# Moving the two-input steps of the projection's GpSimd share to VectorE in a hybrid SGU, convolution and RWKV7 block

## The chip, the cores and the metric

The kernel runs on one core of a Trainium2 chip. The time is that of one execution on the device, in microseconds (us), and a kernel is described by the median of several executions. The engines are TensorE (PE in the rows, PEld for its weight loads), VectorE (DVE), ScalarE (ACT), GpSimd (POOL) and SyncE (SP, which issues the DMAs). A queue works its instructions off in order: one that waits holds all that stand behind it on its engine.

## The reference

The block takes 2048 tokens of width 1024, normalises them, projects them to 29 x 128 columns, feeds three branches, and projects back:

```python
h = rms_norm(x, pre_norm_g[i])
z = h @ w_in[i]                                   # 1024 x 3712
out_a = spatial_gating(u_a, v_a, ...) * silu(g_a)
out_b = conv_module(val_b, glu_b, ...) * silu(g_b)        # 31-tap depthwise convolution
out_c = rwkv7_mix(z[..., oc:og], ...) * silu(z[..., og:]) # token shift, low-rank decay, scan
mix = concatenate([out_a, out_b, out_c]) @ w_out[i]
x = x + rms_norm(mix, post_norm_g[i])
gate = sigmoid(x @ ple_gate_w[i] + ple_gate_b[i])
x = x + (p[i] @ ple_w[i]) * gate
```

All is float32. The change is in how the operands of `z = h @ w_in` and of the low-rank step of `rwkv7_mix` are made ready.

## The kernel before

**Products in two parts.** To keep float32 accuracy, each operand is split in a high part, the value cast to the matmul's own format (a copy on ScalarE), and a low part, the value minus the high part. A product is then the sum of high x high, high x low and low x high. For one column tile (128 columns) over one half of the tokens (1024) that makes 2 groups of 512 tokens x 8 blocks x 3 products = 48 matmuls of 128x512 at line L300 (`gemm1`), some 11.2 us of PE.

**Loops.** The projection runs in two halves of 1024 tokens, each over 29 column tiles in the order of the list `ORDER`. In the first half, `load_w` loads a tile's weights (L278), casts the high part on ScalarE (L282), makes the low part (L283) and writes both to DRAM; in the second half `again` reads them back. Weights and parts share the buffers of the tag "w", six of them, two parts per tile. So the low part of a tile can be written when the gemm of the tile two places before it in `ORDER` has ended, and the load of its raw weights starts when the one three places before has. Accumulators (tag "z") have two buffers: the tile two places on may start when all that read the accumulator are done, for a shifted tile ScalarE's L329, VectorE's L330 and ScalarE's L336.

**Tokens.** The normalised tokens h come in four groups of 512. Group 0 is transposed on PE. Groups 1 to 3 are loaded transposed and scaled (L268), then split (L269, L270). `norm_h` puts the engine for L268 into the tuple `X[g]`: VectorE for group 2, GpSimd for groups 1 and 3.

**What stands around it.** While the projection runs, VectorE works off the 31-tap convolution (L443, then 30 steps L452 for each of two channel tiles and half), the token shift (L330) and the preparation of the RWKV7 operands for four pairs of heads (L469 to L553). The latter has chains across engines: ScalarE's L231 and VectorE's L232 split a tensor, L240 sums it on PE, VectorE's L245 takes reciprocals, and products (L505 to L553) follow. The low-rank part is split at L429 and L430. At the end of the second half L240 (on PE), L637 (ScalarE), L245 and L641 (VectorE) normalise the convolution's output.

**What sets the order.** Each step carries a priority (`at`, or the number that a generator yields, in units of column tiles), and a scheduler with a modelled timeline puts every engine's instructions in order from these priorities and its own idea of durations. The order on all engines can therefore change when a step changes engine. From the last six tiles of the second half on, PE's and VectorE's order is written by hand.

**What GpSimd does.** L165 (two lora weights' low parts), L268 for groups 1 and 3, L283, L430; besides them memsets, the copies L857 and L858, and the products L978 and L1108 of later stages.

Of the kernel before, what the change touches and what calls it, by code (L numbers as in the profile page):

```python
# [14 lines left out]
ALU = mybir.AluOpType  # L15
# [19 lines left out]
def hybrid_kernel(ctx, tc, x, x_t, w_in, vecs, wup, pw_w, sgu_wt, sgu_lnb, sgu_b,  # L35
# [115 lines left out]
    def s_const():  # L151
        yield -0.3
        nc.sync.dma_start(out=swt, in_=sgu_wt)
        nc.gpsimd.memset(swt[64:128, :, 0:64], 0.0)
        lnb = new("mk", (128, 256))
        nc.sync.dma_start(out=lnb, in_=sgu_lnb.partition_broadcast(128))
        sbr = new("mk", (1, 512))
        nc.sync.dma_start(out=sbr, in_=sgu_b)
        wup_t = new("mk", (128, 512))
        nc.sync.dma_start(out=wup_t, in_=wup)  # L160
        for j in range(2):
            hi = slice(64 * j, 64 * j + 64)
            for lo in (0, 64):
                nc.scalar.copy(wup_h[lo:lo + 64, j], wup_t[hi])
            nc.gpsimd.tensor_tensor(out=wup_l[hi], in0=wup_t[hi], in1=wup_h[hi, j], op=ALU.subtract)  # L165
        nc.sync.dma_start(out=pw_t, in_=pw_w.rearrange("(k p) n -> p k n", p=128))
        yield 1.5
        cps = mps((128, 2, 128))
        for hd in range(4):
            ct, lo = hd // 2, 64 * (hd % 2)  # L170
            nc.tensor.matmul(cps[lo:lo + 64, ct, :], lhsT=lnb[:, hd * 64:hd * 64 + 64], rhs=swt[:, hd, :],
                             start=True, stop=False)
            nc.tensor.matmul(cps[lo:lo + 64, ct, :], lhsT=mask[0:1, 64:128], rhs=sbr[:, hd * 128:hd * 128 + 128],
                             start=False, stop=True)
        nc.vector.tensor_copy(out=cmat, in_=cps)
# [12 lines left out]
    def norm_h(g):  # L188


        xt = []
        if g == 0:
            for i in range(4):
                if i == 1:
                    yield
                xi = new("L")
                nc.sync.dma_start(out=xi, in_=x[i * 128:(i + 1) * 128, :])
                junk = new("mk")
                rs = sb.tile([128, 2], F32, tag="rs1", bufs=2, name=nm("rs"))
                nc.scalar.activation(junk, xi, AF.Square, accum_out=rs[:, 0:1])  # L200
                rstd(rs[:, 1:2], rs[:, 0:1], 1.0 / D, 0, 1)
                nc.vector.tensor_scalar(out=xi, in0=xi, scalar1=rs[:, 1:2], scalar2=None, op0=ALU.mult)
                xt.append(xi)
            X[g] = xt
            return
        ssq = sb.tile([128, 4], F32, tag="ssq", bufs=2, name=nm("ssq"))
        for i in range(4):
            xi = new("L")
            nc.sync.dma_start(out=xi, in_=x[(4 * g + i) * 128:(4 * g + i + 1) * 128, :])
            nc.scalar.activation(xi, xi, AF.Square, accum_out=ssq[:, i:i + 1])  # L210
        rs = sb.tile([128, 4], F32, tag="rs", bufs=2, name=nm("rs"))
        rstd(rs, ssq, 1.0 / D, 0, 4)
        rb = new("mk", (128, 2, 512))
        rt = rb[:, 0].rearrange("p (i t) -> p i t", t=128)
        nc.vector.tensor_copy(out=rt, in_=rs.unsqueeze(2).to_broadcast([128, 4, 128]))
        tp = mps(tag="c")
        for i in range(4):
            nc.tensor.transpose(tp[:, i * 128:(i + 1) * 128], rt[:, i, :], ident)
        nc.scalar.copy(rb[:, 1], tp)
        for k2 in range(4):  # L220
            yield
            xk = new("L", (128, 2, 512))
            nc.sync.dma_start(out=xk, in_=x_t[256 * k2:256 * k2 + 256, g * 512:(g + 1) * 512]
                              .rearrange("(k p) t -> p k t", p=128))
            xt += [xk[:, 0], xk[:, 1]]
        X[g] = (xt, rb[:, 1], nc.vector if g % 2 == 0 else nc.gpsimd)

    def parts(src, eng):

# [17 lines left out]
    def build_h(xr, t):  # L247

        h = new("h", (128, 2, 8, 512), F32R)
        if len(xr) == 4:  # L250
# [11 lines left out]
                    nc.scalar.copy(h[:, 0, k4, sl], xb)  # L262
                    nc.vector.tensor_tensor(out=h[:, 1, k4, sl], in0=xb, in1=h[:, 0, k4, sl], op=ALU.subtract)
            return h
        xt, rb, eng = xr
        for k in range(8):
            at(t + 0.05 * k)
            eng.tensor_tensor(out=xt[k], in0=xt[k], in1=rb, op=ALU.mult)  # L268
            nc.scalar.activation(h[:, 0, k, :], xt[k], AF.Identity, scale=col(V_PRE + k))  # L269
            nc.vector.scalar_tensor_tensor(out=h[:, 1, k, :], in0=xt[k], scalar=col(V_PRE + k),  # L270
                                           in1=h[:, 0, k, :], op0=ALU.mult, op1=ALU.subtract)
        return h

    def load_w(*cts, tag="w"):
# [5 lines left out]
        for wr, ct in zip(wrs, cts):  # L280
            ws = [new("w", dt=F32R) for _ in range(2)]
            nc.scalar.copy(ws[0], wr)  # L282
            nc.gpsimd.tensor_tensor(out=ws[1], in0=wr, in1=ws[0], op=ALU.subtract)  # L283
            for j in range(2):
                nc.sync.dma_start(out=w_s[ct, :, j], in_=ws[j].bitcast(F32))
            r.append(ws)
# [130 lines left out]
    def s_lora(half, st):  # L417
# [8 lines left out]
        for j, tag in enumerate(("pg", "mk")):  # L426
            wa = new(tag, dt=F32R)
            hi, lo = slice(64 * j, 64 * j + 64), slice(64 - 64 * j, 128 - 64 * j)
            nc.scalar.copy(wa[hi], o[hi])  # L429
            nc.gpsimd.tensor_tensor(out=wa[lo], in0=o[hi], in1=wa[hi], op=ALU.subtract)  # L430
            st["wa"].append(wa)

    def s_conv(half, ct, st):
# [918 lines left out]
```

## Time and profile before

| | us |
|---|---|
| median of 3 runs | 1438.82 (1437.01 to 1440.38) |
| the profiled execution | 1437.73 |
| its span, first to last instruction | 1436.0 |
| PE busy | 1378.8 |
| VectorE busy | 1009.2 |
| ScalarE busy | 568.6 |
| GpSimd busy | 246.0 |

The mean granted clock of PE is 0.987 of full speed. Busy time is the sum over a whole execution. Which engine the others wait for changes from stretch to stretch, and so the views by stretch and the timelines are read beside it. In a timeline a row gives the start, the length of a group of like instructions from its first to its last end, and in brackets the idle time ahead of it and what ended that.

### The profile page before, as it was taken

How to read it: one execution, taken by the hardware profiler on the slowest of the kernel's cores; microseconds unless marked ns; L12 is line 12 of the kernel's file. 1: busy time of each engine (PE TensorE's matmuls, PEld its weight loads, DVE VectorE, ACT ScalarE, POOL GpSimd, SP SyncE). 2: the span in 40 equal slices, each digit the busy share in tenths (PEclk: the TensorE clock that was granted, in tenths of full speed). 3: DMA queues.
4: the chain of work that ended last, by engine and by line, in shares of the span. 5: the costliest groups of instructions: out<-in, count | busy, mean ns of one | idle time of the engine just before them, and what ended most of it. 6: DMA issues, size and time to landing. Idle time of an engine off the chain costs nothing.

```text
span 1436.0 us, 24389 instructions
## 1 busy us (share of the span) xinstructions
PE 1378.8 (96%) x9701; PEld 1102.1 (77%) x9701; DVE 1009.2 (70%) x2003; ACT 568.6 (40%) x897; POOL 246.0 (17%) x284
## 2 busy tenths in 40 slices
PE   7999999999999999999898999999998999999998
PEld 6876877887898778778676777777776777888887
DVE  6599994885537999777667588678779544545453
ACT  6334444555332343453433443544543543111121
POOL 5442221221501000000111211211221101111120
PEclk9999999999999999999899899999999999999999
DMA  8432465679534558855723833242331534242331
GB/s 335 148 147 88 150 212 181 191 277 286 208 116 153 175 175 241 231 153 192 227 89 121 291 113 95 76 140 82 109 100 56 169 124 153 99 139 99 118 117 44
DMA packets 158311, 223.29 MB, mean 155 GB/s; under 512 B 58236, under 2 KB 108149, under 8 KB 158198
## 3 DMA queue, kind: packets, MB, share of 16 engines
q1 hardware_dynamic: 158066, 221.68, 46.9%
q8 instruction: 76, 1.25, 0.4%
q14 instruction: 37, 0.30, 0.1%
q10 hardware_dynamic: 132, 0.06, 0.0%
HBM read 132.58 MB, written 89.13 MB: 154 GB/s over the span
## 4 chain that ended last, share of the span: by engine, by line
PE 73%; DVE 20%; ACT 3%; issue 2%; DMA 1%; DVEq 0%; ACTq 0%
PE z L300 33%; PE z L1164 12%; PE z L1051 8%; DVE inv L452 5%; PE c L1141 3%; PE z L312 3%; DVE inv L873 3%; PE m L820 3%; DVE inv L878 2%; PE m L240 1%; DVE mk L245 1%; DVE inv L861 1%; PE m L1120 1%; DVE L L976 1%; DMA w<-in_gate_w_dram 1%
## 5 line engine op out<-in xcount | busy, mean ns | idle before, releaser
L300 PE MATMUL z<-h,w 128*128 128x512 f32 x2592 | 630.5, 398 | 0.0
L300 PEld LDWEIGHTS z<-h,w 128*128 128x128 f32 x2592 | 484.0, 189 | 118.0 <-issue 6.4
L1051 PE MATMUL z<-h,w 128*128 128x512 f32 x768 | 206.0, 412 | 0.7 <-DVE w L1038 0.7
L452 DVE SCALAR_TENSOR_TENSOR inv<-inv,vc,inv 128x1024 f32<-128x1024 f32 x120 | 173.0, 1460 | 1.4
L1051 PEld LDWEIGHTS z<-h,w 128*128 128x128 f32 x768 | 139.9, 192 | 31.7 <-DVE w L1038 1.1
L283 POOL TENSOR_TENSOR w<-w,w 128x1024 fp32r<-128x1024 f32 x26 | 74.3, 2857 | 235.9 <-PE z L300 178.1
L1164 PE MATMUL z<-L,w 128*128 128x512 f32 (+1 forms) x384 | 96.3, 394 | 0.0
L1164 PE MATMUL z<-h,w 128*128 128x512 f32 (+1 forms) x384 | 93.1, 390 | 0.8 <-DVE inv L1147 0.8
L1148 ACT ACTIVATE inv<-inv 128x512 f32<-128x512 f32 (+1 forms) x33 | 20.4, 620 | 181.7 <-DVE inv L1147 181.7
L873 DVE TENSOR_TENSOR inv<-inv,inv 128x48 f32<-128x48 f32 (+23 forms) x464 | 85.8, 219 | 2.3
L878 DVE TENSOR_TENSOR inv<-inv,inv 128x48 f32<-128x48 f32 (+23 forms) x464 | 84.3, 217 | 1.2
L1164 PEld LDWEIGHTS z<-h,w 128*128 128x128 f32 x384 | 71.3, 188 | 17.4 <-DVE inv L1147 1.2
L1147 DVE TENSOR_TENSOR inv<-z,L 128x512 f32<-128x512 f32 (+1 forms) x32 | 21.9, 683 | 87.8 <-PE z L1164 87.8
L1164 PEld LDWEIGHTS z<-L,w 128*128 128x128 f32 x384 | 70.4, 188 | 15.3
L1108 POOL TENSOR_TENSOR inv<-inv,pg 128x1024 f32<-128x1024 f32 x16 | 38.3, 2394 | 216.9 <-DMA inv<-mx_s 117.6
L245 DVE RECIPROCAL mk<-mk 128x256 f32<-128x256 f32 x40 | 65.8, 1708 | 12.1 <-ACT mk L637 8.0
L825 DVE TENSOR_TENSOR mk<-m,mask 128x512 f32<-128x512 f32 x58 | 37.6, 685 | 35.9 <-PE m L820 31.4
L978 POOL TENSOR_TENSOR ri<-ri,pc 128x256 f32<-128x256 f32 x31 | 19.5, 630 | 236.8 <-DVE L L976 226.6
L829 ACT COPY inv<-mk 32x128 f32<-32x128 f32 x128 | 37.8, 295 | 52.9 <-DVE mk L825 50.1
L820 PE MATMUL m<-L,L 64*128 64x128 f32 x464 | 44.5, 299 | 10.1 <-DVE yn L1002 8.6
L312 PE MATMUL z<-w,h 128*128 128x256 f32 x384 | 52.6, 293 | 0.9 <-ACT h L262 0.9
L312 PEld LDWEIGHTS z<-w,h 128*128 128x128 f32 x384 | 50.3, 197 | 3.1 <-ACT h L262 1.6
(244 smaller groups left out, 1932.9 us busy)
## 6 DMA issues: line engine op xcount, KB each, us to landing
w_s<-w SPq DMA_DIRECT2D x58, 512.0 KB, 3.3
w<-w_s SPq DMA_DIRECT2D x58, 512.0 KB, 5.4
w<-in_w_in_dram SPq DMA_DIRECT2D x26, 512.0 KB, 3.5
L<-in_x_dram SPq DMA_DIRECT2D x16, 512.0 KB, 7.3
ar_s<-L SPq DMA_DIRECT2D x16, 512.0 KB, 5.0
wo_s<-w SPq DMA_DIRECT2D x16, 512.0 KB, 4.2
L<-ar_s SPq DMA_DIRECT2D x32, 256.0 KB, 3.1
L<-bk_s SPq DMA_DIRECT2D x32, 256.0 KB, 4.1
```

What stands on the lines that cost most here:

```text
L245: nc.vector.reciprocal(t[:, g * 256:(g + 1) * 256], t[:, g * 256:(g + 1) * 256])
L283: nc.gpsimd.tensor_tensor(out=ws[1], in0=wr, in1=ws[0], op=ALU.subtract)
L300: nc.tensor.matmul(z[:, g * 512:(g + 1) * 512], lhsT=ws[a][:, k * 128:(k + 1) * 128], rhs=h[:, b, k, :], start=(n == 0), stop=(n == 23))
L312: nc.tensor.matmul(z[:, i * 256:(i + 1) * 256], lhsT=h[:, b, k, i * 128:(i + 1) * 128], rhs=ws[k // 4][a][:, (k % 4) * 256:(k % 4 + 1) * 2 ...
L452: nc.vector.scalar_tensor_tensor(out=ac, in0=y[:, i:i + HT], scalar=col(V_CW + 2 * i + ct), in1=ac, op0=ALU.mult, op1=ALU.add)
L820: nc.tensor.matmul(sp[par][:, p, :], lhsT=bk[lo:lo + 64, p, :], rhs=ar[lo:lo + 64, p, :], start=True, stop=True)
L873: nc.vector.tensor_tensor(out=tmp[:, o:o + n, :m], in0=tl[:, lo:hi, m:m + 1].to_broadcast([128, n, m]), in1=ml[:, m, :m].unsqueeze(1).to_b ...
L878: nc.vector.tensor_tensor(out=tl[:, lo:hi, :m], in0=tl[:, lo:hi, :m], in1=tmp[:, o:o + n, :m], op=ALU.add)
L1051: nc.tensor.matmul(mx[:, nh * 512:(nh + 1) * 512], lhsT=oT[a][:, k, :], rhs=wo[k // 4][:, b, k % 4, nh * 512:(nh + 1) * 512], start=(k == ...
L1108: nc.gpsimd.tensor_tensor(out=x2, in0=x2, in1=pg[0], op=ALU.mult)
L1141: nc.tensor.matmul(pp, lhsT=pT[:, a, k, :], rhs=gw[8 + k][b][:, nh * 512:(nh + 1) * 512], start=(n == 0), stop=(n == 5))
L1164: nc.tensor.matmul(z, lhsT=xT[a][:, k, :], rhs=gw[k][b][:, sl], start=(k == 0 and n == 0), stop=(k == 7 and n == 2))
```

## The change

Four kinds of two-input steps are issued on VectorE where they were issued on GpSimd: the low parts of the lora weights (L165, 2 instructions), the scaling of token groups 1 and 3 (L268, 16 instructions), the low parts of the column weights (L283, 29 instructions) and those of the low-rank part (L430, 4 instructions). The arithmetic is the same. `X[g]` no longer carries an engine.

```diff
@@ s_const
-            nc.gpsimd.tensor_tensor(out=wup_l[hi], in0=wup_t[hi], in1=wup_h[hi, j], op=ALU.subtract)
+            nc.vector.tensor_tensor(out=wup_l[hi], in0=wup_t[hi], in1=wup_h[hi, j], op=ALU.subtract)
@@ norm_h
-        X[g] = (xt, rb[:, 1], nc.vector if g % 2 == 0 else nc.gpsimd)
+        X[g] = (xt, rb[:, 1])
@@ build_h
-        xt, rb, eng = xr
+        xt, rb = xr
         for k in range(8):
             at(t + 0.05 * k)
-            eng.tensor_tensor(out=xt[k], in0=xt[k], in1=rb, op=ALU.mult)
+            nc.vector.tensor_tensor(out=xt[k], in0=xt[k], in1=rb, op=ALU.mult)
@@ load_w
-            nc.gpsimd.tensor_tensor(out=ws[1], in0=wr, in1=ws[0], op=ALU.subtract)
+            nc.vector.tensor_tensor(out=ws[1], in0=wr, in1=ws[0], op=ALU.subtract)
@@ s_lora
-            nc.gpsimd.tensor_tensor(out=wa[lo], in0=o[hi], in1=wa[hi], op=ALU.subtract)
+            nc.vector.tensor_tensor(out=wa[lo], in0=o[hi], in1=wa[hi], op=ALU.subtract)
```

The scheduler's order moves in three places that matter below. The number behind a name tells tensors apart; z_n is the accumulator of a column tile, m_n and c_n are small accumulators, mk_n and L_n are tensors of 128x1024, w_n are weights and their parts. In the first half, tiles come in the order z_1104, z_1171, z_1247, z_1369, z_1446, z_1569, z_1636, z_1721.

On PE, at the end of z_1104, the sums L240 on m_1054 (first key pair) before:

```order
L300 MATMUL z_1104<-h_289,w_922 128x512
L240 MATMUL m_1054<-mk_1050,ones_83 128x512
L240 MATMUL m_1058<-mk_1050,ones_83 128x512
L300 MATMUL z_1104<-h_289,w_922 128x512
L469 MATMUL c_1082<-mk_766,ri_122 128x512
L474 MATMUL c_1082<-mk_766,yc_123 128x512
L300 MATMUL z_1104<-h_289,w_923 128x512
```

and after:

```order
L300 MATMUL z_1104<-h_289,w_923 128x512
L469 MATMUL c_1082<-mk_766,ri_122 128x512
L474 MATMUL c_1082<-mk_766,yc_123 128x512
L300 MATMUL z_1171<-h_224,w_987 128x512 x2
L300 MATMUL z_1171<-h_224,w_988 128x512
L240 MATMUL m_1054<-mk_1050,ones_83 128x512
L240 MATMUL m_1058<-mk_1050,ones_83 128x512
```

The first L240 has moved behind all of z_1104 and the first three matmuls of z_1171.

On VectorE, at the second key pair (mk_1300), before:

```order
L330 SCALAR_TENSOR_TENSOR L_1419<-z_1369,vc,L_1419 128x1023
L452 SCALAR_TENSOR_TENSOR inv_894<-inv_890,vc,inv_894 128x1024 x2
L501 TENSOR_SCALAR mk_1300<-m_1306 128x512
L501 TENSOR_SCALAR mk_1300<-m_1310 128x512
L452 SCALAR_TENSOR_TENSOR inv_894<-inv_890,vc,inv_894 128x1024
L245 RECIPROCAL mk_1300<-mk_1300 128x256 x4
```

and after:

```order
L546 SCALAR_TENSOR_TENSOR L_979<-L_979,vc,L_1044 128x1024
L452 SCALAR_TENSOR_TENSOR inv_894<-inv_890,vc,inv_894 128x1024 x2
L283 TENSOR_TENSOR w_1428<-w_1425,w_1427 128x1024
L501 TENSOR_SCALAR mk_1300<-m_1306 128x512
L501 TENSOR_SCALAR mk_1300<-m_1310 128x512
L452 SCALAR_TENSOR_TENSOR inv_894<-inv_890,vc,inv_894 128x1024 x2
L245 RECIPROCAL mk_1300<-mk_1300 128x256 x4
L452 SCALAR_TENSOR_TENSOR inv_894<-inv_890,vc,inv_894 128x1024
L232 TENSOR_TENSOR mk_1353<-L_979,mk_1352 128x1024
L283 TENSOR_TENSOR w_1547<-w_1544,w_1546 128x1024
```

The low part w_1428, of the tile whose accumulator is z_1636, now stands ahead of this pair's L501 and L245, and w_1547, of z_1721, behind its L232.

On PE, at the end of the scheduled part of the second half (z_4922 is its last tile), before:

```order
L240 MATMUL m_4741<-mk_4737,onesm 128x512
L240 MATMUL m_4747<-mk_4737,onesm 128x512
L300 MATMUL z_4922<-h_2839,w_4650 128x512
L300 MATMUL z_4922<-h_2839,w_4649 128x512 x2
L300 MATMUL z_4922<-h_2839,w_4650 128x512
L300 MATMUL z_4922<-h_2839,w_4649 128x512 x2
L300 MATMUL z_4922<-h_2839,w_4650 128x512
L300 MATMUL z_4922<-h_2839,w_4649 128x512 x2
L300 MATMUL z_4922<-h_2839,w_4650 128x512
L300 MATMUL z_4922<-h_2839,w_4649 128x512
L537 MATMUL m_4833<-ident,L_4724 128x128 x4
```

and after:

```order
L300 MATMUL z_4922<-h_2839,w_4650 128x512
L300 MATMUL z_4922<-h_2839,w_4649 128x512
L240 MATMUL m_4741<-mk_4737,onesm 128x512
L240 MATMUL m_4747<-mk_4737,onesm 128x512
L537 MATMUL m_4833<-ident,L_4724 128x128 x4
```

The eleven matmuls of z_4922 that stood between L240 and L537 now stand ahead of L240.

## Rows read from the trace of the kernel before

**Rows 1.** The page's engines: busy us, share of the span, instructions.
```profile
PE 1378.8 (96%) x9701; PEld 1102.1 (77%) x9701; DVE 1009.2 (70%) x2003; ACT 568.6 (40%) x897; POOL 246.0 (17%) x284
```

**Rows 2.** Busy by stretch: length, PE, PEld, DVE, ACT, POOL (count); clock, DMA share, GB/s.
```profile
67.30:220.70 153.40, 148.91 (x624) 116.02 (x623) 152.46 (x116) 66.27 (x76) 41.88 (x16) 0.98 0.46 154
...
140.50:147.50 7.00, 6.16 (x13) 4.21 (x14) 6.96 (x6) 4.56 (x6) 0.80 (x1) 0.51 0.00 0
...
194.60:225.30 30.70, 29.44 (x124) 21.85 (x123) 27.95 (x24) 20.95 (x24) 7.25 (x4) 1.00 0.75 219
...
225.00:450.00 225.00, 225.00 (x1101) 182.78 (x1101) 130.45 (x139) 92.41 (x114) 44.75 (x21) 1.00 0.62 206
```

**Rows 3.** GpSimd's groups: out<-in, shapes, count, busy us, mean ns, idle before.
```profile
L283 POOL TENSOR_TENSOR w<-w,w 128x1024 fp32r<-128x1024 f32 x26 | 74.3, 2857 | 235.9 <-PE z L300 178.1 <-ACT w L282 46.1 <-DMA bk_s<-mk 8.2
...
L268 POOL TENSOR_TENSOR L<-L,mk 128x512 f32<-128x512 f32 x16 | 26.0, 1656 | 13.6 <-DMA w_s<-w 13.6
```

**Rows 4.** VectorE's timeline, 137 to 221 us: start, us, instruction.
```profile
137.69 1.27 DVE L330 SCALAR_TENSOR_TENSOR L<-z,vc,L 128x1023 f32<-128x1023 f32 x1
...
162.90 0.68 DVE L517 TENSOR_TENSOR L<-L,L 128x512 f32<-128x512 f32 x1
163.50 1.27 DVE L452 SCALAR_TENSOR_TENSOR inv<-inv,vc,inv 128x1024 f32<-128x1024 f32 x1
164.70 1.27 DVE L330 SCALAR_TENSOR_TENSOR L<-z,vc,L 128x1023 f32<-128x1023 f32 x1
...
168.89 1.21 DVE L521 TENSOR_TENSOR mk<-mk,mk 128x1024 f32<-128x1024 f32 x1
170.03 3.43 DVE L452 SCALAR_TENSOR_TENSOR inv<-inv,vc,inv 128x1024 f32<-128x1024 f32 x1
...
214.93 2.31 DVE L481 TENSOR_TENSOR_SCAN L<-inv,L 128x1040 f32<-128x1040 f32 x1
...
220.68 1.27 DVE L330 SCALAR_TENSOR_TENSOR L<-z,vc,L 128x1023 f32<-128x1023 f32 x1
```

**Rows 5.** GpSimd's timeline at the same place.
```profile
169.44 2.93 POOL L283 TENSOR_TENSOR w<-w,w 128x1024 fp32r<-128x1024 f32 x1 [8.74 <-PE z L300]
```

**Rows 6.** PE's timeline at three places of the first half.
```profile
133.04 4.91 PE L300 MATMUL z<-h,w 128*128 128x512 f32 x20
141.34 1.22 PE L240 MATMUL m<-mk,ones 128*128 128x512 f32 x2 [3.38 <-ACT mk L231]
...
193.59 1.17 PE L300 MATMUL z<-h,w 128*128 128x512 f32 x4
...
225.29 3.17 PE L300 MATMUL z<-h,w 128*128 128x512 f32 x13
```

**Rows 7.** VectorE's timeline at the end of the second half's scheduled part.
```profile
687.35 6.59 DVE L245 RECIPROCAL mk<-mk 128x256 f32<-128x256 f32 x4 [6.14 <-ACT mk L637]
```

**Rows 8.** ScalarE's timeline ahead of 225 us.
```profile
223.63 1.03 ACT L231 CAST mk<-L 128x1024 fp32r<-128x1024 f32 x1
...
224.69 0.15 ACT L336 COPY zl<-z 128x1 f32<-128x1 f32 x1
```

**Rows 9.** PE's timeline at the end of the second half's scheduled part.
```profile
686.20 0.61 PE L240 MATMUL m<-mk,onesm 128*128 128x512 f32 x2
686.65 2.73 PE L300 MATMUL z<-h,w 128*128 128x512 f32 x11
689.22 1.03 PE L537 MATMUL m<-ident,L 128*128 128x128 f32 x8
...
697.93 1.34 PE L603 MATMUL m<-yc,mk 128*64 128x128 f32 x10 [1.64 <-DVE L L553]
```

**Rows 10.** PE's waits from 0 to 67.3 us: total us, times, longest.
```profile
PE m L259 <- DVE L L202: 2.2, 1, 2.2
```

**Rows 11.** The weights' loads (line L278): from issue to landing.
```profile
DMA to landing us min/median/max: 3.4/3.7/7.3
```

## The prediction, as it was put on record

> **What bounds the kernel now.** The first view is the engines' busy time on the profile's page [rows 1]: TensorE (PE) is busy for 1378.8 of 1436.0 us, VectorE (DVE) for 1009.2. Read alone, this says that DVE has 427 us to spare and that a little more work there costs nothing. The second view, busy time by stretch [rows 2], says where that is false. From 67.3 to 220.7 us DVE is busy for 152.46 of 153.40 us, while PE has already lost 4.5 us. From 225 to 450 us PE is busy in every microsecond and DVE for only 130.45 of 225. So DVE decides before 221 us and PE decides after that, and the change is worth something only where DVE decides, or where a chain passes from engine to engine.
>
> The third view, GpSimd's groups (POOL) [rows 3], shows the price of the steps where they are: 2857 ns for a low part of 128x1024, 1656 ns for a 128x512 scaling step. The fourth, the timeline of DVE and of POOL at 162 to 174 us, shows that these prices are not POOL's alone. The convolution step L452 takes 1.27 us when POOL is idle and 3.43 us when POOL's low part runs, which itself takes 2.93 us [rows 4, 5]. Most of what POOL does here is taken from DVE.
>
> The Trainium skill, page "SBUF — State Buffer", section "Who interferes with whom", says that a VectorE instruction with two inputs in SBUF contends with a GpSimd instruction that reads SBUF, and that the one that comes second is blocked to the end of the first. The 3.43 us beside 2.93 us agree with that.
>
> The fifth view, PE's timeline [rows 6], shows the largest loss in that stretch: PE stops at 137.95 (133.04 + 4.91) and goes on at 141.34, 3.38 us, because L240 needs a product that stands behind DVE's L330 of 137.69. Behind the pause the granted clock is 0.51 from 140.5 to 147.5 us, the lower of its two levels (1.2 of 2.4 GHz), with 6.16 us busy [rows 2]: 6.16 x 0.49 = 3.0 us more. That stall costs 6.4 us in all.
>
> **The change, part by part.** Between 67.3 us, where the convolution begins, and L330 of z_1569, which starts at 220.68 in the trace [rows 4], 14 steps move to DVE: 12 low parts and 2 low-rank parts. Alone on DVE, a two-input product over 128x1024 lasts 1.14 us from its start to the next (168.89 to 170.03), a scalar-tensor-tensor step 1.20 (163.50 to 164.70), a 128x512 step 0.60 (162.90 to 163.50). The 116 DVE instructions of this stretch [rows 2], summed by these durations and those of their other forms, give 129.6 us, where the trace took 153.3: 23.7 us were lost to POOL's reads. After the change the sum is 144.3 us, 14.7 more, with nothing of POOL's in the way. So DVE gains 9 us over this stretch, if it never waits.
>
> *The stall at 138.* By sums DVE reaches the L330 in front of it some 5 to 10 us sooner, and the new PE order sets L240 on m_1054 later: behind all 48 matmuls of z_1104 and 3 of z_1171, where before 5 matmuls of z_1104 were still to come. I take the whole stall as gone: -6.4 us, and -1 for the short waits behind it. z_1446's last matmul, 194.6 in the trace (193.59 and about 1) [rows 6], then comes at 187.2.
>
> *What is late next.* On POOL a low part waited for its buffer and held up nobody. On DVE it waits at the head of the queue, and all that stands behind it waits too. w_1428 can be written only when the gemm of z_1446 has ended, for its buffer was that tile's. It stands ahead of L501, L245 and the rest of this key pair. From there to the end of L330 on z_1569, which frees the accumulator of z_1721, DVE has in its new order 9 products of 1.14, 11 steps of 1.20, 7 of 0.60, four reciprocals that take 6.6 [rows 7] and a scan of 2.3 [rows 4]: 10.3 + 13.2 + 4.2 + 6.6 + 2.3 = 36.6 us. It ends at 187.2 + 36.6 = 223.8 at the earliest. PE's work over the same piece is 29.44 us busy of 30.7 before [rows 2], so PE runs dry near 216 and idles some 8 us. ScalarE's L336, which also frees that accumulator, is now behind one more cast (about 1.03, by L231's row) [rows 8]; before it ended at 224.84. I take 225.1 for z_1721's first matmul, against 225.29 in the trace: the 9 us of DVE are spent waiting at w_1428 and its neighbours, and the net is -0.2. The bounds are 223.8 (-1.5) and 226.5 (+1.2, one more cast).
>
> *The clock.* The pause of 3.38 us brought the clock down; the waits of about 1 us in 194.6 to 225.3 did not, as that row has 1.00 [rows 2]. A pause of 8 us should. The price is that of the first one, +3.0 us (bounds 0 and 3.5), now behind 225 us, where PE has no idle time to make it good.
>
> *The end of the scheduled projection.* In the old order 11 matmuls of z_4922 stand between L240 on mk_4737 and L537; they fill PE while ScalarE's L637, DVE's four L245 and L232 work [rows 7, 9]. In the new order these 11 stand ahead of that L240, and nothing stands between. The chain from 686.20 to L603 at 697.93 is 11.7 us long whatever PE does in it, so it starts 11 x 0.234 = +2.6 us later (11 matmuls in 2.55 us, from 686.65 to 689.22). The bounds are 0, if DVE's part of this chain was ready late anyway, and 2.6.
>
> *The start.* Six low parts, the two lora parts and 8 scalings come to DVE's queue before 67 us: 6.8 + 1.2 + 4.8 us at most on an engine with idle time. PE waits 2.2 us for DVE's L202 there [rows 10]. Against that, h of the second token group comes sooner. I take 0, bounds -1.5 and +1.5, from that row.
>
> *The rest.* The other 11 low parts, 8 scalings and 2 low-rank parts lie behind 221 us, where DVE has 95 us free of the 225 up to 450 and PE none; they cost nothing as long as loads are on time. If that cover goes, a low part costs its 1.14 us. From about 700 us on, the order of PE, DVE and POOL is the same.
>
> The sum: -0.2 + 3.0 + 2.6 + 0 = +5.4 us on the profiled execution's 1437.7, so **1443**. The median of the runs shown is 1438.8, 1.1 above that execution; this goes into the range.
>
> **The rivals.**
> *Faster: DVE keeps its lead.* If the low parts' buffers are free when DVE gets to them, the 9 us carry through, PE does not run dry at 216, and the stall at 138 is gone for good: -6.4 + 2.6 = -3.8, 1433.9. For it: POOL too waited for PE's gemm, 178.1 us in all before its low parts [rows 3], and PE lost nothing by that. Against it: 36.6 us of DVE work against 29.4 of PE's, behind one gate. It decides if less than about 29 us stand behind w_1428.
>
> *The same: the pause moves but costs no clock.* Then -0.2 + 2.6 = +2.4, 1440.1; with the end's term at 0 also, 1437.5. A way to this result too: DVE's 152.46 busy us include the time in which it was blocked, so that POOL's work was already paid for on DVE, and taking it over openly frees nothing there; then the stall at 138 stays and only the end's term counts, 1437.7 to 1440.3. The Trainium skill, page "Perfetto Trace Analysis", section "Optimizing Scalar/DVE Operations", says that moving work between these two engines might not help, as they share a read port. Here the 23.7 us lost against 14.7 added speak against this as far as DVE's sum goes, but for it in that the gain may buy nothing.
>
> *Slower still: late loads hold DVE.* A weight's load lands in 3.7 us in the median and in 7.3 at worst [rows 11]. A late one used to hold POOL; now L330 of the previous tile is behind it in some places, and with it PE. One or two of them after 225 us cost 3.6 to 7.2 us where PE has no slack: 1446.7 to 1450.
>
> *The change does nothing it says.* The new order has every one of the 51 steps on DVE, so I give this no chance.
>
> **How the numbers follow.** The forecast gets 0.50 (its own range 1441.7 to 1446), slower still 0.12, the same 0.26, faster 0.12. A measurement of this kernel tells about 0.2%, 2.9 us, from no change, so faster means under 1435.9 and slower over 1441.7: 0.12, 0.26, 0.62. The range takes the forecast and the same, with the lower edge 1436 above the faster case, and goes up to 1449, into the late loads: some 0.16 is left out.
>
> **What would show it.** Right: no pause at 138 and a clock of 1.00 at 140 to 147; L452 at 1.2 to 1.3 us throughout; DVE waiting for PE ahead of w_1428; PE idle for some microseconds before 225 with a clock near 0.5 behind it; L603 later by 2.6 us than by the shift at 686 alone. Wrong: PE busy from 190 to 225 with z_1721 starting at 219 or so (the faster rival), or L300 waiting for late loads after 225 us (the slower one). The end's term falls if L240 on mk_4737 waits for DVE.

## The result and the profile after

| | before | changed |
|---|---|---|
| median of the runs, us | 1438.73 (1437.01 to 1440.38, 4 runs) | 1451.87 (1448.66 to 1455.17, 4 runs) |
| profiled execution, us | 1437.73 | 1455.17 |
| its span, us | 1436.0 | 1453.5 |
| mean granted clock | 0.987 | 0.980 |

The ratio of changed to before is 1.0089, with a 95% interval of 1.0066 to 1.0112: slower by 13.1 us. The direction was forecast; the time lies above the range (1436 to 1449). The changed kernel was run once more in another series, against 29 runs of the kernel before: ratio 1.0081 (1.0058 to 1.0104). Its median there is 1450.2 us over five runs; a sixth, of 3383 us, fell in the chip's slow state and is left out.

The page of the changed kernel, first its engines [rows 1], then the groups of the convolution step and of the low part:

```profile
PE 1384.7 (95%) x9701; PEld 1107.1 (76%) x9701; DVE 1005.8 (69%) x2054; ACT 572.9 (39%) x899; POOL 124.3 (9%) x233
...
L452 DVE SCALAR_TENSOR_TENSOR inv<-inv,vc,inv 128x1024 f32<-128x1024 f32 x120 | 150.8, 1275 | 1.2
...
L283 DVE TENSOR_TENSOR w<-w,w 128x1024 fp32r<-128x1024 f32 x26 | 31.7, 1220 | 29.0 <-PE z L300 10.8
```

The convolution step on the page of the kernel before:

```profile
L452 DVE SCALAR_TENSOR_TENSOR inv<-inv,vc,inv 128x1024 f32<-128x1024 f32 x120 | 173.0, 1460 | 1.4
```

VectorE has 51 instructions more and is busy for 3.4 us less. L452 fell from a mean of 1460 ns in the profile before to 1275, which over 120 instructions is 22 us given back, and a low part costs 1.22 us where it cost GpSimd 2.86 [rows 3]. As far as the work goes, the change does what was read from [rows 4, 5]. The Trainium skill, page "Perfetto Trace Analysis", section "Optimizing Scalar/DVE Operations", says that moving work between these two engines might not help; on VectorE's own time the trace differs, and whether it helps the whole is a matter of what follows.

Where the time went can be read by setting the start of one and the same matmul in both traces side by side. All shifts below are worked out so: start in the kernel named minus start in the kernel before, us, each from one profiled execution. The three kernels on the right come from the experiments. How much one execution carries can be seen in a kernel of the experiments (all square roots first) that has the order of the kernel before up to 839 us: its shifts up to there lie between -2.2 (z_1247) and +1.9 us.

```
first matmul of          before   changed  shift | two square  no low-rank  low-rank of
                                                 | roots back  parts        2nd half only, roots back
z_1104 (first half)       126.83    126.23  -0.6 |   -1.0         +0.1         -0.8
z_1247                    158.23    151.27  -7.0 |   -7.3         -6.2         -7.1
z_1569                    195.59    186.28  -9.3 |   -9.7         -8.1         -9.0
z_1636                    209.17    202.94  -6.2 |   -6.6         -8.4         -9.1
z_1721                    225.29    228.65  +3.4 |   +3.0         -6.7         -7.2
the tile behind it        239.00    243.72  +4.7 |   +4.2         -6.6         -7.4
a tile of the 2nd half    462.04    467.91  +5.9 |   +4.4         -3.1         -3.7
z_4922                    676.69    682.48  +5.8 |   +4.3         -3.1         -3.8
the tile behind it        708.54    716.42  +7.9 |   +6.6         -3.8         -1.3
L1051, first              818.08    824.99  +6.9 |   +5.6         -4.9         -1.3
L1164, first             1195.36   1212.62 +17.3 |   +5.0         -0.9         -1.3
```

There are four steps: a gain of 7 us at 138, a loss of 14 from z_1569 to the tile behind z_1721, a loss of 2 at the end of the projection's scheduled part, and a loss of 10 between 818 and 1195 us. (z_4922 is the first tile whose own matmuls are ordered by hand, not the last of the scheduled ones, as the text ahead has it.)

The first is plain in the windows of the changed kernel (length, then busy PE, PEld, DVE, ACT, POOL, clock, DMA share, GB/s):

```profile
67.30:223.30 156.00, 148.78 (x629) 116.47 (x627) 146.66 (x129) 66.55 (x75) 0.26 (x2) 0.98 0.48 157
140.50:147.50 7.00, 7.00 (x32) 5.68 (x31) 7.00 (x8) 4.59 (x7) 0.00 (x0) 1.00 0.51 208
194.60:228.60 34.00, 23.96 (x91) 17.34 (x90) 30.55 (x27) 21.48 (x25) 0.13 (x1) 0.84 0.65 185
```

At 140 to 147 us PE has no gap and the full clock, against 6.16 us busy and 0.51 before [rows 2]. In 194.6 to 228.6 it is busy for 24 of 34 us, at 0.84. PE's timeline shows the three pauses:

```profile
202.94 6.23 PE L300 MATMUL z<-h,w 128*128 128x512 f32 x19 [3.54 <-ACT mk L592]
...
224.31 0.80 PE L469 MATMUL c<-mk,ri 128*128 128x512 f32 x1 [4.69 <-ACT mk L478]
225.04 0.79 PE L474 MATMUL c<-mk,yc 64*128 64x512 f32 x1
227.62 1.22 PE L240 MATMUL m<-mk,ones 128*128 128x512 f32 x2 [1.80 <-ACT mk L231]
228.65 4.54 PE L300 MATMUL z<-h,w 128*128 128x512 f32 x13
```

Each of the three ends with ScalarE, not with VectorE. ScalarE's timeline around them:

```profile
200.57 1.28 ACT L592 ACT_TABLE_LOAD   x1 [3.96 <-DMA v_s<-mk]
...
217.23 0.59 ACT L539 COPY mk<-m 128x512 f32<-128x512 f32 x1 [4.02 <-PE m L537]
...
223.57 0.69 ACT L478 ACTIVATE mk<-c,vc 128x512 f32<-128x512 f32 x1
...
225.57 1.07 ACT L485 ACTIVATE L<-L 128x1040 f32<-128x1040 f32 x1
226.54 1.03 ACT L231 CAST mk<-L 128x1024 fp32r<-128x1024 f32 x1
```

L592 waits for a buffer that the DMA of the transposed v frees. That v is transposed on PE by L537, which stands 35 matmuls of L300 later in the new order (late in z_1446 before, inside z_1569 now). The second pause ends with L478, in an unbroken run of ScalarE's that starts at 217.23 with the copies (L539) of what another L537 transposed; that one stands 28 matmuls later than before. And z_1721 stands behind L240, which waits for L231, at the end of the same run.

VectorE holds z_1721 too. Its accumulator is that of z_1569, which L330 reads. VectorE's timeline from the low part w_1428 to that L330:

```profile
186.31 1.23 DVE L283 TENSOR_TENSOR w<-w,w 128x1024 fp32r<-128x1024 f32 x1 [1.49 <-PE z L300]
...
223.31 1.27 DVE L330 SCALAR_TENSOR_TENSOR L<-z,vc,L 128x1023 f32<-128x1023 f32 x1
```

So z_1721 could not start before 224.58 whatever ScalarE did; L240 makes it 4.1 us later.

The end of the projection [rows 9], PE's timeline of the changed kernel:

```profile
694.56 0.62 PE L240 MATMUL m<-mk,onesm 128*128 128x512 f32 x2
695.73 1.24 PE L537 MATMUL m<-ident,L 128*128 128x128 f32 x8 [0.55 <-ACT mk L637]
698.01 0.98 PE L240 MATMUL m<-mk,ones 128*128 128x512 f32 x2 [1.04 <-ACT mk L231]
703.43 1.22 PE L240 MATMUL m<-mk,ones 128*128 128x512 f32 x2 [4.44 <-DVE mk L232]
706.30 1.12 PE L603 MATMUL m<-yc,mk 128*64 128x128 f32 x8 [1.64 <-DVE L L553]
```

The chain from the last L240 on `onesm` to L603 is 11.7 us, as before; the 11 matmuls that filled it are gone, and PE waits 4.44 us where it waited 2.65 in the kernel before:

```profile
695.07 1.22 PE L240 MATMUL m<-mk,ones 128*128 128x512 f32 x2 [2.65 <-DVE mk L232]
```

The step is small beside the scatter of one execution, but it stands in every profile with this order (1.6 to 2.5 us, eight of them) and in none of the seven without it (-1.0 to 0).

The last loss was not in the forecast at all. The late stage, which works off 16 blocks of tokens, has on PE, VectorE and GpSimd the same order in both kernels. On ScalarE it has not: at two of the blocks the square root L999 stood ahead of the copies L952 and L953, and now stands behind them. (Besides these, one L993 near 1100 us has moved by a place.) ScalarE's timeline of the kernel before at the first of the two:

```profile
996.60 0.30 ACT L999 ACTIVATE grs<-grs,epsr 128x8 f32<-128x8 f32 x1 [0.86 <-DVE grs L998]
996.81 0.35 ACT L952 COPY L<-c 64x256 f32<-64x256 f32 x1
997.18 0.37 ACT L953 COPY L<-c 64x256 f32<-64x256 f32 x1
```

and of the changed kernel at the same block:

```profile
1004.52 0.37 ACT L952 COPY L<-c 64x256 f32<-64x256 f32 x1 [0.59 <-PE c L949]
1004.91 0.37 ACT L953 COPY L<-c 64x256 f32<-64x256 f32 x1
1005.30 0.30 ACT L999 ACTIVATE grs<-grs,epsr 128x8 f32<-128x8 f32 x1
```

VectorE's L1002 comes behind L999, and PE's L820 behind L1002. PE's waits, of the kernel before from 990 to 1065 us:

```profile
PE m L820 <- DVE yn L1002: 2.9, 2, 1.4
```

and of the changed kernel from 1000 to 1075, which is the same work:

```profile
PE m L820 <- DVE yn L1002: 3.8, 2, 1.9
```

That is 0.45 us more at each of the two. The matmuls behind it tell the rest, in PE's timeline before:

```profile
998.14 1.13 PE L820 MATMUL m<-L,L 64*128 64x128 f32 x14 [1.44 <-DVE yn L1002]
```

and after:

```profile
1006.78 2.04 PE L820 MATMUL m<-L,L 64*128 64x128 f32 x14 [1.89 <-DVE yn L1002]
```

The same 14 matmuls take 2.04 us instead of 1.13: the clock has fallen to its lower level (1.2 of 2.4 GHz). Over 990 to 1065 us the kernel before had a clock of 1.00, and the changed kernel has 0.91 in the window that answers to it. At these two blocks the shift grows by 3.5 and 3.35 us, 6.9 of the 9.2 us by which it grows between 976 and 1130 us; the rest are drops of the clock at other places.

### The profile page after: what moved, and what is told of

Its sections match the earlier page's. It is cut to its first block, busy times and chain, and to the rows that moved or that the text cites. A ratio compares the mean times of both kernels' runs of the same rounds, so it can differ in the third digit from the quotient of the medians.

```text
span 1453.5 us, 24373 instructions
## 1 busy us (share of the span) xinstructions
PE 1384.7 (95%) x9701; PEld 1107.1 (76%) x9701; DVE 1005.8 (69%) x2054; ACT 572.9 (39%) x899; POOL 124.3 (9%) x233
## 4 chain that ended last, share of the span: by engine, by line
PE 81%; DVE 12%; ACT 4%; DMA 2%; issue 1%; SPq 0%; DVEq 0%; ACTq 0%
PE z L300 41%; PE z L1164 12%; PE z L1051 8%; PE z L312 3%; PE c L1141 3%; DVE inv L873 3%; DVE inv L878 3%; PE m L820 3%; PE m L240 1%; DVE inv L861 1%; PE m L1120 1%; DVE L L976 1%; PE c L943 1%; PE c L474 1%; PE c L931 1%
## 5 line engine op out<-in xcount | busy, mean ns | idle before, releaser
L300 PE MATMUL z<-h,w 128*128 128x512 f32 x2592 | 631.0, 399 | 4.8 <-ACT mk L592 3.5
L300 PEld LDWEIGHTS z<-h,w 128*128 128x128 f32 x2592 | 485.5, 189 | 123.5 <-issue 7.2
L452 DVE SCALAR_TENSOR_TENSOR inv<-inv,vc,inv 128x1024 f32<-128x1024 f32 x120 | 150.8, 1275 | 1.2
L245 DVE RECIPROCAL mk<-mk 128x256 f32<-128x256 f32 x40 | 65.9, 1709 | 20.7 <-ACT mk L503 11.7
L329 ACT ACTIVATE L<-z,om 128x1024 f32<-128x1024 f32 x24 | 26.8, 1116 | 85.1 <-PE z L300 85.1
L282 ACT CAST w<-w 128x1024 fp32r<-128x1024 f32 x26 | 27.3, 1051 | 81.8 <-DMA w<-in_w_in_dram 61.8
L820 PE MATMUL m<-L,L 64*128 64x128 f32 x464 | 44.4, 300 | 11.1 <-DVE yn L1002 9.5
L283 DVE TENSOR_TENSOR w<-w,w 128x1024 fp32r<-128x1024 f32 x26 | 31.7, 1220 | 29.0 <-PE z L300 10.8
```

The source lines that it names most:

```text
L245: nc.vector.reciprocal(t[:, g * 256:(g + 1) * 256], t[:, g * 256:(g + 1) * 256])
L300: nc.tensor.matmul(z[:, g * 512:(g + 1) * 512], lhsT=ws[a][:, k * 128:(k + 1) * 128], rhs=h[:, b, k, :], start=(n == 0), stop=(n == 23))
L452: nc.vector.scalar_tensor_tensor(out=ac, in0=y[:, i:i + HT], scalar=col(V_CW + 2 * i + ct), in1=ac, op0=ALU.mult, op1=ALU.add)
L820: nc.tensor.matmul(sp[par][:, p, :], lhsT=bk[lo:lo + 64, p, :], rhs=ar[lo:lo + 64, p, :], start=True, stop=True)
```

## The experiments

Theory A: the late loss comes from the two swapped square roots, by way of the clock. Theory F, formed when the parts had been run: the projection's losses come from the order that the four low-rank instructions (L430) bring about, not from the low parts that wait on VectorE. The rivals are in the expectations. Ratios are to the kernel before on the same chip, with 95% intervals.

### The square roots put back

An ordering edge between two ScalarE instructions, without a semaphore, puts L999 ahead of the copies of the block that follows. For chosen blocks:

```diff
+SQ_FIRST, DEP = (8, 10, 12), (mybir.DependencyClass.NoSync, mybir.DependencyReason.DATA)
+def behind_sqrt(tc, F, cp): (q := F.pop("sq", (-1, 0)))[0] in SQ_FIRST and tc.add_manual_dep(cp.ins, q[1].ins.name, mybir.DependencyInfo(*DEP))
...
-        nc.scalar.copy(uv[0:64, 0, :], up[0:64].rearrange("p q d -> p (q d)"))
+        behind_sqrt(tc, F, nc.scalar.copy(uv[0:64, 0, :], up[0:64].rearrange("p q d -> p (q d)")))
...
-        nc.scalar.activation(grs, grs, AF.Sqrt, scale=1.0 / 64.0, bias=epsr[:, 2:3])
+        F["sq"] = t, nc.scalar.activation(grs, grs, AF.Sqrt, scale=1.0 / 64.0, bias=epsr[:, 2:3])
```

> The changed kernel, with two ScalarE instructions put back where they stood before: at two chunks of the late stage the square root L999 again goes ahead of the copies L952 and L953. The order of PE, VectorE and GpSimd is that of the changed kernel. Theory A (the late loss comes from these two swaps: PE waits 0.45 us longer for L1002 there, and the clock falls behind that longer wait): the 9.5 us that the profiled execution lost between 1000 and 1150 us go, and about 1445 us are left (1438.7 plus the 6 to 8 us of the projection). Rival B (the late loss is where clock drops happen to fall, whatever the order): no change, 1449 to 1455. Rival C (only the two waits count, not the clock): 1 us less, about 1451.

Measured: 1445.47 us (1442.92 to 1447.80, 8 runs), ratio 1.0041 (1.0028 to 1.0054). Two instructions in another place on an engine that is 39% busy take away 6.4 us, and the interval does not touch that of the changed kernel. Theory A gave 1445. The shift in the table's column of this kernel goes from 5.6 to 5.0 us in the late stage. Rivals B (1449 to 1455) and C fell: the two waits alone are 0.9 us.

The same edge on the kernel before, at all blocks from 2 to 12:

> The kernel before, with the square root L999 ahead of the copies L952 and L953 at all chunks of the late stage, where it was ahead at two chunks of ten and behind at eight. Theory A: eight waits of PE get 0.45 us shorter (3.6 us) and with the shorter waits the clock drops at 895 us and its like go (1.7 us each): 1431 to 1435. Rival B: 1.7 to 3.6 us at the most from the shorter waits, with clock drops as before: 1435 to 1438. Rival D (the wait is not on the path that ends last): 1438.7, no change.

Measured: 1434.93 us (7 runs), ratio 0.9967 (0.9954 to 0.9981): 5.3 us faster, at the end of theory A's range, with a rise of the mean clock from 0.987 to 0.989. It is the unchanged kernel with eight square roots moved by two places. Who waited for L1002, over the whole execution (total us, times), in the kernel before and in this one:

```profile
  PE m L820: 8.6, 5
```

```profile
  PE m L820: 6.9, 5
```

These waits are shorter by 1.7 us in all, not by the 3.6 that theory A counted.

On the changed kernel the other eight were put first too:

> The changed kernel with the square roots L999 ahead of the copies at all chunks. Theory A: another 5 us less than with two of them put back (1445.5): 1439 to 1442. If the clock drops of the late stage fall elsewhere instead of going: 1443 to 1445.

Measured: 1442.14 us (12 runs), ratio 1.0020 (1.0009 to 1.0031), 3.3 us less than with two, where 5 were expected.

The late stage by itself, 830 to 1165 us, one row for each kernel; the last number but two is the clock. Before, changed, changed again, two roots back, all roots first on the kernel before:

```profile
830.00:1165.00 335.00, 311.85 (x4071) 246.86 (x4070) 259.52 (x974) 155.20 (x327) 59.28 (x118) 0.99 0.34 108
```

```profile
830.00:1165.00 335.00, 312.22 (x3950) 247.27 (x3949) 254.85 (x992) 150.41 (x317) 59.08 (x118) 0.95 0.32 103
```

```profile
830.00:1165.00 335.00, 310.31 (x4001) 246.38 (x4000) 259.67 (x999) 150.52 (x317) 59.40 (x118) 0.97 0.34 106
```

```profile
830.00:1165.00 335.00, 313.94 (x4087) 248.62 (x4085) 262.81 (x1003) 157.38 (x329) 59.63 (x118) 0.98 0.34 109
```

```profile
830.00:1165.00 335.00, 313.91 (x4093) 249.03 (x4092) 260.40 (x981) 156.34 (x331) 59.33 (x118) 0.99 0.34 108
```

PE gets 3950 matmuls done in 335 us in the one case and 4071 to 4093 in others, at nearly the same busy time: what differs is the clock. 0.04 of clock over 335 us is half speed for 27 us, 13 us lost.

These rows are of one execution each, and the two that matter most lie at opposite ends: the profiled execution of the changed kernel is the slowest of its four, that with two roots back the fastest of its eight. The mean clock of every run is on record. Over nine runs of the changed kernel it is 0.982, over the eight with two roots back 0.983; one minus the clock, times the time, gives 25.5 us against 24.8. So the clock accounts for less than 1 of the 6.4 us in the mean of the runs. In the two other pairs of this section it accounts for more: 3.0 of 5.3 us on the kernel before, and 4.6 us where 3.3 were measured, from two roots to all. That the place of the square roots costs time is shown, since these edits move nothing else; that most of it goes by the clock is seen in the profiled executions, and in the mean of the changed kernel's runs it is not shown.

> The changed kernel once more, for its spread and a second profile. All theories: 1448 to 1455. Theory A expects again a clock drop at one of the two chunks near 1006 and 1061 us or at both; a theory in which they fall anywhere expects none there in particular.

Measured: 1450.2 us, as said above. In its profile the clock fell at one of the two places that theory A named and also at others that it did not: the shift grows there by 0.4 and 2.0 us, against 3.4 at each in the first profile, and by 5.6 us over the late stage, against 10.4. Counted over all sixteen profiles, the clock falls at these two blocks in 6 of 9 cases where the root stands behind the copies, and in 7 of 23 where it stands ahead. So the longer wait goes with more drops; it doesn't fix where they come.

### The parts of the change

Each of the four kinds of steps can be moved or left out by itself.

> Only the low parts of the column weights (L283) go to VectorE; the lora weights, the scaling of token groups 1 and 3 and the low-rank parts stay on GpSimd. In the order that comes out, the square roots of the late stage stand as in the kernel before. Theory A: the loss of the first half is that of the changed kernel (about 4 to 5 us at 240 us), the late loss is absent: about 1443 to 1446. Rival B: as slow as the changed kernel, 1449 to 1455, give or take where the clock drops fall.

Measured: 1447.16 us (6 runs), ratio 1.0045 (1.0028 to 1.0062). The sum fits neither number well, and both theories were wrong on its way: at 240 us this kernel is 4.3 us ahead, not behind. It loses 9 us at the end of the first half, by a wait that no other kernel has:

```profile
383.09 1.22 PE L300 MATMUL z<-h,w 128*128 128x512 f32 x2 [6.10 <-DVE w L283]
```

There, the last tile's low part stands on VectorE behind eight steps L268 of group 2, which GpSimd's L268 of group 3 stretch:

```profile
368.29 12.54 DVE L268 TENSOR_TENSOR L<-L,mk 128x512 f32<-128x512 f32 x8 [8.18 <-ACT mk L219]
380.76 2.28 DVE L283 TENSOR_TENSOR w<-w,w 128x1024 fp32r<-128x1024 f32 x1
```

So the forecast's fear, a low part at the wrong place of VectorE's queue, is real. It comes when only a part of the work is moved, and at another place.

> The lora weights, the scaling of token groups 1 and 3 and the low-rank parts go to VectorE, the low parts of the column weights (L283) stay on GpSimd. Theory A: L283 still takes VectorE's port, the pause at 138 us and its half clock stay, and nothing waits at a low part; the square roots stand ahead of the copies at three chunks, one more than before: 1436 to 1440. Rival E (what is lost in the first half comes from the scaling and the low-rank parts on VectorE): 1443 or more.

Measured: 1443.34 us (11 runs), ratio 1.0024 (1.0014 to 1.0034), 3.1 us slower, and out of theory A's range at the upper end. Its square roots stand ahead of the copies at three blocks, as many as in the kernel before, but two of them are others; at the second of the two blocks above it has the swap. This kernel has the step at the end of the projection (+1.8 us there). That pointed to the low-rank parts, since the kernel with the low parts alone has no such step.

> The change without its fourth part: the low-rank parts (L430, 4 instructions) stay on GpSimd, all else goes to VectorE as in the change. In the order that comes out, the square roots L999 stand as before, 11 matmuls stand again between L240 and L537 at the end of the scheduled projection, and L240 of the third key pair stands inside z_1721 and not ahead of it. Theory F (the loss comes by way of the order that the four low-rank instructions bring about, at three places): the first half gains 4 to 6 us at 240 us, nothing is lost at the end of the projection or behind 1000 us: 1433 to 1437. Rival G (the low parts on VectorE cost what the forecast said, +3 at 240 us): 1441 to 1444.

Measured: 1438.05 us (1433.26 to 1442.27, 12 runs), ratio 0.9991 (0.9976 to 1.0007). With 47 of the 51 instructions moved, the loss is gone. In the first half PE is 6.6 us ahead at the tile behind z_1721 (column "no low-rank parts" of the table), as theory F has it, and rival G is out. The time is not the 1433 to 1437 expected: of the 3.8 us left at 708 us, the profiled execution gives 2.9 back in the late stage, at a clock of 0.97 there. PE's timeline at the place where the changed kernel stands still:

```profile
217.78 0.50 PE L469 MATMUL c<-mk,ri 128*128 128x512 f32 x1 [2.39 <-ACT mk L478]
218.22 0.49 PE L474 MATMUL c<-mk,yc 64*128 64x512 f32 x1
218.64 3.71 PE L300 MATMUL z<-h,w 128*128 128x512 f32 x10
```

One pause of 2.4 us is left of three, and z_1721 starts at once behind L474: in this order L240 stands inside z_1721, and waits for nothing there. It can start because VectorE is through with L330 on z_1569 earlier:

```profile
187.49 1.23 DVE L283 TENSOR_TENSOR w<-w,w 128x1024 fp32r<-128x1024 f32 x1
...
216.82 1.27 DVE L330 SCALAR_TENSOR_TENSOR L<-z,vc,L 128x1023 f32<-128x1023 f32 x1
```

From the low part w_1428 to the end of that L330 are 30.6 us here and 38.3 in the changed kernel, where L526, L546, two L501 and two more L452 stand between. So of the 10.0 us between the two kernels at z_1721, 6.5 lie in VectorE's order and 3.5 in L240's place on PE.

> Only the low-rank parts (L430, 4 instructions) go to VectorE. In the order that comes out, the square roots L999 stand behind the copies at both places, as in the changed kernel, and no matmul stands between L240 and L537 at the end. Theory F: +2 us at the end of the projection and +4 to +9 us behind 1000 us: 1445 to 1451, the larger part of the change's loss from 4 of its 51 instructions. Rival G: 1438 to 1441, since 4 instructions of about 1.1 us cannot matter.

Measured: 1447.45 us (1440.33 to 1451.55, 11 runs), ratio 1.0052 (1.0036 to 1.0069): four instructions of some 1.2 us each cost 7.5 us. The profiled execution happens to be the fastest of the eleven, so its trace shows only 2.6 us of it, 1.6 of them at the end of the projection. In the first half these four alone lose next to nothing (+0.4 us behind z_1721, +2.4 in the profile of the next kernel): the loss there needs the low parts on VectorE as well. With the two square roots put back:

> Only the low-rank parts (L430) go to VectorE, and the two square roots stand as in the kernel before. What is left is the end of the projection, where no matmul stands between L240 and L537. Theory F with A: +2 us from there: 1440 to 1442, some 6 us less than the 1447.5 with the swaps. Rival (the 7.5 us of the low-rank parts have another cause): 1445 to 1448.

Measured: 1442.32 us (12 runs), ratio 1.0021 (1.0006 to 1.0036). By the medians 5.1 us were the swaps, by the ratios 4.5 of 7.5; the two intervals meet at 1.0036. The profiles don't show it: over the late stage the shift grows by 1.3 us in the one with the swaps, and by 6.0 in this one, which is the second slowest of its twelve.

A pair that differs in three square roots (and in two neighbours L1109 that change places on VectorE at 1127 us), and has no step in the projection:

> Only the scaling of token groups 1 and 3 (L268, 16 instructions) goes to VectorE. From the second column tile on, PE's order is that of the kernel before, but on ScalarE the square roots L999 come out behind the copies at all ten chunks (and at one more behind). Theory A (the swaps cost, wherever they come from): nothing in the projection, +4 to +7 us behind 1000 us: 1443 to 1446. Rival B (the order of the two does not matter): 1438 to 1440.

Measured: 1441.74 us (12 runs), ratio 1.0019 (1.0006 to 1.0032).

> The same, with three square roots put back where the kernel before has them, and no other instruction in another place. Theory A: 1437 to 1440, and some 5 us less than its twin. Rival B: as its twin, within 1 us.

Measured: 1440.43 us (12 runs), ratio 1.0011 (0.9995 to 1.0028). The twin is 1.3 us faster, which the intervals don't tell from nothing; 5 were expected, and under 1 by rival B. The swap's price is therefore 6.4, 5.1 and 1.3 us in three pairs, the last for three roots; it is clear of noise in the first and not shown in the last.

### The two halves of the low-rank parts

What was open was whether two instructions make the first half's loss and the other two that at the end. In the changed kernel, with the square roots as before:

```diff
-            nc.vector.tensor_tensor(out=wa[lo], in0=o[hi], in1=wa[hi], op=ALU.subtract)
+            (nc.gpsimd if half == 0 else nc.vector).tensor_tensor(out=wa[lo], in0=o[hi], in1=wa[hi], op=ALU.subtract)
```

> The changed kernel with the two low-rank parts of the first half on GpSimd (those of the second half stay on VectorE), and the square roots L999 as in the kernel before. In the first half the order is that of the change without its low-rank parts; at the end of the projection still no matmul stands between L240 and L537. Theory F (two low-rank parts in VectorE's first half make PE's order there, and that order costs 10 us between 187 and 240 us): PE's shift against the kernel before is -4 to -7 us at 240 us where the changed kernel has +4.7, and +2 us come at the end of the projection: 1437 to 1441, against 1445.5 with all low-rank parts on VectorE. Rival G (the first half's loss comes from the low parts, not from the order): 1444 to 1446.

Measured: 1436.28 us (8 runs), ratio 0.9975 (0.9963 to 0.9987): faster than the kernel before by 4 us, with 49 of 51 instructions moved. The last column of the table has both parts of the expectation, each a little over: -7.4 us behind z_1721, and +2.5 at the end of the projection (-3.8 to -1.3). The other way round (`half == 1` in the line above):

> The changed kernel with the two low-rank parts of the second half on GpSimd (those of the first half stay on VectorE), the square roots as in the kernel before but first at two more chunks. The first half's order is that of the changed kernel; at the end of the projection 11 matmuls stand again between L240 and L537. Theory F: +4.5 us at 240 us as in the changed kernel, nothing more at the end: 1442 to 1444, some 2 to 3 us under 1445.5. Rival (the end's 2.1 us have another cause): 1445 to 1446, and the shift steps up by 2 us at L603 as before.

Measured: 1441.15 us (11 runs), ratio 1.0009 (0.9995 to 1.0023). Its profile has +6.2 us behind z_1721, and no step at the end (+7.8 to +7.4). The time is 1 to 3 us under the expectation; it has the square root first at two more blocks than the kernel that it is held against. Both losses of the projection are thus shown to come with two instructions each, given the low parts on VectorE. Which of the places that these two change costs what is read from the timelines; no run moves one place alone.

### A version that beats both

The change without the low-rank parts, and the square roots first at all blocks from 2 to 12:

> The change without the low-rank parts, and with the square roots L999 ahead of the copies at all chunks. Theory F with theory A: the gain of the first half (4 us) and that of the shorter waits of the late stage (5.3 us as measured on the kernel before) add up: 1429 to 1432, faster than the kernel before and than the kernel before with the square roots first. If the first half's gain is not there (rival G): 1436 to 1439.

Measured: 1431.43 us (1428.88 to 1433.74, 6 runs), ratio 0.9947 (0.9930 to 0.9965): 7.7 us faster than the kernel before and 20 faster than the changed one.

## Why the prediction was right and wrong

The forecast was 1443; the changed kernel takes 1452. With the two square roots where they were it takes 1445.5, inside the forecast's own range. The signs of being right that it named came (no pause at 138, a wait at w_1428, PE idle ahead of 225, L603 later), and none of them looks at the late stage. That 1445.5 lies so near is in part luck: the first half lost 4.7 us for 2.8, by another way than was worked out. By its steps:

- **VectorE's prices**: right. 1.22 us busy for a low part, 1.275 for L452, and a VectorE that is busy for 146.7 us of the stretch with the steps more. (14 steps at 1.14 are 16.0 us, where the forecast adds 14.7; L430 too takes 1.22 on VectorE.)
- **The stall at 138 us**: right, gone, and z_1569 starts at 186.3 where 187.2 was worked out for the end of the tile ahead of it. The shift is -7.0 us at z_1247 (-6.4 forecast). That the clock's 3.0 us count in full was not so: in the kernel before with all square roots first, which has the same order here, the clock did not fall there; it is 3.4 us ahead at z_1247 (+1.2 to -2.2) and has lost that again at z_1569 (+0.3).
- **36.6 us of VectorE behind w_1428**: right as a sum. In the trace that low part starts at 186.31, after a wait of 1.49 us for the gemm, and L330 on z_1569 ends at 224.58: 38.3 us with 1.7 of waits.
- **z_1721 at 225.1, upper bound 226.5**: wrong, 228.65. The step put 1.3 us between the end of L330 and this tile, for L336; it is 4.1. L336 doesn't hold the tile (without the low-rank parts it starts at 220.28, behind z_1721's 218.64). PE's own order does: L240 stands ahead of it and waits for L231 on ScalarE. The earlier pauses, for L592 and L478, were not seen either. Over the first half the net is +4.7 us behind z_1721, clock included, against +2.8.
- **That the low parts cause it**: wrong as far as it goes by them alone. Without the low-rank parts the same low part waits at the same gate, and PE gains 6.6 us. The faster rival named this ("VectorE keeps its lead"), with the condition of less than about 29 us behind w_1428: 30.6 us stand there in that kernel and 38.3 in the changed one. So the amount of work behind the gate did count, as the forecast has it, and the order that the two low-rank parts bring sets it; L240's place on PE adds 3.5 us, which was not seen.
- **The clock, +3.0 us (0 to 3.5)**: too low, 4.4. At 0.84 over 34 us, 10.9 us run at half speed, in some 5 of which PE is idle: about 3 us are lost, and 1.4 more behind z_1721's start, where the shift grows from 3.4 to 4.7.
- **The end of the projection, +2.6 us**: right, +2.1 here, and it goes when the second half's two low-rank parts go back.
- **The start, 0**: right within its bounds (-0.6, and +1.3 in the second profile).
- **"From about 700 us on, the order of PE, DVE and POOL is the same"**: this is the step that failed. The sentence is true and leaves out ScalarE, where two square roots had changed places with four copies. That the stage was the same was read from three engines of four, and so it was costed at nothing; it cost 6.4 us as a median, and 10 in the profiled execution.
- **The range**: it had 1.1 us for the distance from the profiled execution to the median, and nothing for how much the clock makes one and the same kernel vary.

## What to carry to other kernels

When a scheduler sets the order, moving an instruction to another engine is two changes: the work, which the rows price well, and a new order everywhere, which has to be compared on all engines to the end of the program; four instructions of some 1.2 us, moved alone, cost 7.5 us here. A small operation that stands between two engines (a square root of 128x8) belongs ahead of copies that nobody waits for as urgently (5.3 us on the kernel before). Test a change in its parts before it is dropped: 49 of these 51 moves were a gain of 0.25% once the late order was held, and the two that spoil it can stay on GpSimd.

## What was not expected of the hardware

A wait of PE that is 0.45 us longer, twice, goes with 6.4 us in the median. In the profiled execution the granted clock fell to its lower level behind both, 14 matmuls took 2.04 us where they had taken 1.13, and each place cost 3.4 us. In the mean of all runs the clock explains less than 1 of the 6.4; what the rest is was not found out. Where the clock falls differs from execution to execution of one kernel. In the kernel before it was 0.51 behind the pause at 138 us; in the kernel that differs from it only from 839 us on (the square roots first) the pause at the same place was 2.67 us in its profiled execution, and the clock was 1.00 from 137 to 149 us. The runs of one kernel spread by up to 11 us (1440.33 to 1451.55 for the low-rank parts alone), so that one profiled execution can stand far from the median. What decides between a drop and none was not found out.
